# RMSNorm with repeated rows: gamma loaded on the loads' own queue, and one VectorE copy in two

## The chip, the cores and the metric

The kernel runs on one core of a Trainium2 chip. The core has five engines with an instruction stream each: TensorE (PE, unused here), VectorE (DVE), ScalarE (ACT), GpSimd (POOL) and SyncE (SP), and sixteen DMA engines that move data between the chip's main memory (HBM) and the on-chip memory of 128 partitions. A DMA is issued from a queue of an engine, SP's (q1 in the profile) or ACT's (q10) here, and is cut into packets that are spread over the DMA engines. Each engine works through its instructions in order and waits on semaphores for the others.

The metric is the time of one execution on the device, in microseconds (us), as the median of several runs.

## What is computed

```python
# x: 8 x 512 x 2048 float32, gamma: 2048 float32
x_rep = np.repeat(x, 2, axis=1)
rms = np.sqrt((x_rep ** 2).mean(axis=-1, keepdims=True) + 1e-6)
return ((x_rep / rms) * gamma[None, None, :]).astype(np.float32)
```

Every row of 2048 values is divided by its root mean square, multiplied by gamma, and written out twice in a row. 33.5 MB are read and 67.1 MB written.

## The kernel before

All 4096 rows are taken in four loads of 1024 rows: each partition gets 8 consecutive rows (64 KB, one contiguous piece of HBM). One load feeds two stores; a store writes 4 rows of each partition, twice each, so again 64 KB per partition. That makes 4 loads and 8 stores, twelve transfers of 128 pieces of 64 KB, all issued by SP in one queue.

On chip there is one tile y of 24 rows per partition, in three areas of 8 rows called `first`, `second` and `third`. `four(n, constants)` handles two loads, and is called twice. It issues load n into rows 4 to 11, then runs `constants()` (which does work in the first call only), then issues load n+1 into `third`. Four groups follow, each of 4 rows per partition:

- `squares` (L57): ACT squares each row and sums it up (L63), then takes the root (L67).
- `scale` (L70): DVE takes the reciprocal (L73), then one operation per row multiplies by it and by `gamma_b` (L75), writing into the even places of the group's area.
- `repeat` (L80): a copy of the even places into the odd ones (L82), by ACT or DVE.
- `store` (L52): SP issues the store (L53).

The first group of a call is done in two halves of 2 rows; its first half is copied by ACT, its second by DVE. In the second group (`second`), ACT copies the second half and DVE the first half, one copy of 4096 elements per partition (L102). The third and fourth group are copied by ACT alone. An area is written again only when the store that reads it has landed: load 2 waits for the third store (and, in the same queue, load 3 for the fourth).

The order of instructions on every engine is the order in which the program issues them (a manual schedule). SP's queue is thus load 0, load 1, four stores, load 2, load 3, four stores; here loads and stores are counted from 0.

`constants()` (L120) brings gamma in and spreads it over the partitions. It issues on ACT's queue one DMA of 16 pieces of 125 values (500 B, L121) and three DMAs of one piece of 16 values (64 B, L127). They go to one partition of y, into rows that no load fills but the first group's scaling writes later; so the first store also waits for these DMAs. Then POOL broadcasts the 2000 values to all partitions of `gamma_b` (L131) and the last 48 (L135). DVE sets the constant eps (L136), and ACT takes a root of it (L139), which also loads ACT's table.

Of the kernel before, what the change touches and what calls it, by code (L numbers as in the profile page):

```python
# [1 line left out]

# [4 lines left out]


@with_exitstack
def kernel(  # L10
    ctx: ExitStack,
    tc: tile.TileContext,
    x: bass.AP,
    gamma: bass.AP,
    out: bass.AP,
):
    nc = tc.nc
    P = nc.NUM_PARTITIONS
    f32 = mybir.dt.float32
    Act = mybir.ActivationFunctionType  # L20
    Alu = mybir.AluOpType

    B, S, D = x.shape
    Bo, So, Do = out.shape
    R = So // S
    assert R == 2 and D == Do and B == Bo and So == S * R
    eps = 1e-6
    inv_d = 1.0 / float(D)


    K = 4
    N = B * S
    ntiles = N // (P * K)
    assert N % (P * K) == 0 and ntiles == 8
    H = 2
    x_t = x.rearrange("b s d -> (b s) d").rearrange("(n p k) d -> n p k d", p=P, k=H * K)
    out_t = out.rearrange("b s d -> (b s) d").rearrange("(n p h j) d -> n h p (j d)", p=P, h=H, j=K * R)

    singles = ctx.enter_context(tc.tile_pool(name="singles", bufs=1))
    rows = ctx.enter_context(tc.tile_pool(name="rows", bufs=1))  # L40
    junk = ctx.enter_context(tc.tile_pool(name="junk", bufs=1, space=bass.MemoryType.PSUM))
    small = ctx.enter_context(tc.tile_pool(name="small", bufs=4))

    y = rows.tile([P, 3 * K * R, D], f32, name="y")
    first, second, third = 0, K * R, 2 * K * R

    def load(n, at):
        nc.sync.dma_start(out=y[:, at : at + H * K, :], in_=x_t[n])  # L50

    def store(n, h, to):  # L52
        nc.sync.dma_start(  # L53
            out=out_t[n, h], in_=y[:, to : to + K * R, :].rearrange("p j d -> p (j d)")
        )

    def squares(at, rows):  # L57

        n = len(rows)
        ss = small.tile([P, n], f32, name=f"ss{n}")  # L60
        for c, k in enumerate(rows):
            sq = junk.tile([P, D], f32, name="sq")
            nc.scalar.activation(  # L63
                out=sq[:], in_=y[:, at + k, :], func=Act.Square, accum_out=ss[:, c : c + 1]
            )
        rms = small.tile([P, n], f32, name=f"rms{n}")
        nc.scalar.activation(out=rms[:], in_=ss[:], func=Act.Sqrt, scale=inv_d, bias=eps_t[:])  # L67
        return rms

    def scale(at, to, rows, rms):  # L70
        n = len(rows)
        rstd = small.tile([P, n], f32, name=f"rstd{n}")
        nc.vector.reciprocal(out=rstd[:], in_=rms[:])  # L73
        for c, k in enumerate(rows):
            nc.vector.scalar_tensor_tensor(  # L75
                out=y[:, to + R * k, :], in0=y[:, at + k, :], scalar=rstd[:, c : c + 1],
                in1=gamma_b[:], op0=Alu.mult, op1=Alu.mult,
            )

    def repeat(to, k0, k1, copy):  # L80
        y_r = y[:, to + R * k0 : to + R * k1, :].rearrange("p (k r) d -> p k r d", r=R)
        copy(out=y_r[:, :, 1, :], in_=y_r[:, :, 0, :])  # L82

    ctx.enter_context(tc.manual_schedule())

    half = K // 2
    up, down = list(range(K)), list(range(K - 1, -1, -1))

    def four(n, constants):


        load(n, first + K)
        constants()
        load(n + 1, third)
        for rows in (up[:half], up[half:]):
            scale(first + K, first, rows, squares(first + K, rows))
        repeat(first, 0, half, nc.scalar.copy)
        repeat(first, half, K, nc.vector.tensor_copy)
        store(n, 0, first)
        scale(second, second, down, squares(second, down))  # L100
        repeat(second, half, K, nc.scalar.copy)
        repeat(second, 0, half, nc.vector.tensor_copy)  # L102
        store(n, 1, second)
        roots = [squares(third + h * K, up) for h in range(H)]
        scale(third, first, up, roots[0])
        repeat(first, 0, half, nc.scalar.copy)
        repeat(first, half, K, nc.scalar.copy)
        store(n + 1, 0, first)
        scale(third + K, third, up, roots[1])
        repeat(third, 0, K, nc.scalar.copy)  # L110
        store(n + 1, 1, third)

    gamma_b = singles.tile([P, D], f32, name="gamma_b")
    G, E = 16, 3
    C = D // G - E
    gamma_s = y[0:1, 0:2, :].rearrange("p k (c d) -> p (k c) d", c=G // 2)
    gamma_t = y[0:1, 2, :]
    eps_t = singles.tile([P, 1], f32, name="eps_t")

    def constants():  # L120
        nc.scalar.dma_start(  # L121
            out=gamma_s[0:1, :, :C],
            in_=gamma[: G * C].rearrange("(p c d) -> p c d", p=1, c=G),
        )
        for c in range(E):
            at = G * C + c * G
            nc.scalar.dma_start(  # L127
                out=gamma_t[0:1, c * G : (c + 1) * G],
                in_=gamma[at : at + G].partition_broadcast(1),
            )  # L130
        nc.gpsimd.partition_broadcast(  # L131
            out_ap=gamma_b[:, : G * C].rearrange("p (c d) -> p c d", c=G),
            in_ap=gamma_s[0:1, :, :C],
        )
        nc.gpsimd.partition_broadcast(out_ap=gamma_b[:, G * C :], in_ap=gamma_t[0:1, : E * G])  # L135
        nc.vector.memset(eps_t, eps)  # L136

        root = singles.tile([P, 1], f32, name="root")[:]
        nc.scalar.activation(out=root, in_=eps_t[:], func=Act.Sqrt)  # L139

    four(0, constants)
    four(2, lambda: None)


# [1 line left out]
_INS = ['x', 'gamma']  # L146
_OUTS = [((8, 1024, 2048), 'float32')]


# [23 lines left out]
```

## Time and profile before

| what | value |
|---|---|
| median of 3 runs (lowest to highest) | 238.42 us (238.42 to 239.19) |
| profiled execution, its own time | 238.52 us |
| its span, first to last instruction | 236.3 us |
| busy: DVE, ACT, POOL | 84.4, 110.2, 2.8 us (36%, 47%, 1% of the span) |
| moved by DMA | 100.68 MB, mean 426 GB/s |
| load 0 issued, landed | 0.72, 22.70 us |
| gamma landed: the 16 pieces, the three small DMAs | 10.59; 15.43, 20.27, 22.88 us |

The profile is of one execution. Its page gives, line by line, the busy time of the engines, the DMA queues (packets, MB, and the time of their packets as a share of sixteen engines' span), a chain of work followed back from the last instruction, and groups of instructions: line, engine, operation, output<-input, count, then busy us and mean ns of one, then the idle time of the engine just before them and what ended most of it. A timeline gives start and duration in us, the engine, and in square brackets the idle time before and its releaser. A table by stretches gives for each stretch its length, then busy time (and count) of DVE, ACT and POOL, the clock of TensorE, the DMA engines' share and GB/s. The trace behind it also has each DMA packet with start, duration and size, and the moment at which each engine's share of a DMA was reported as landed; a completion packet of 4 B follows the data of each DMA on each engine.

### The profile page before, as it was taken

The page shows a single profiled execution, that of the slowest core. Times are in us where ns is not written, and L with a number is a line of the kernel's source. Part 1 is how long each engine was busy: PE and PEld are TensorE (multiplying, and loading weights), DVE is VectorE, ACT ScalarE, POOL GpSimd, SP SyncE. Part 2 cuts the span into 40 slices and gives each one's busy share as a digit, 9 for nine tenths or more (in the row PEclk, how much of TensorE's full clock was granted, in tenths as well). Part 3 has the DMA queues.
Part 4 walks back from the last instruction along what each step waited for, and adds up shares of the span by engine and source line. Part 5 has one row for each costly group of instructions (what it writes and reads, how often), then busy time and mean ns, then how long its engine had stood idle before and what let it go on. Part 6 is the DMA issues. An engine that isn't in the chain of part 4 may idle for free.

```text
span 236.3 us, 225 instructions
## 1 busy us (share of the span) xinstructions
DVE 84.4 (36%) x47; ACT 110.2 (47%) x86; POOL 2.8 (1%) x6
## 2 busy tenths in 40 slices
DVE  0000396594699500000000007929919992000000
ACT  2001989479998470000000049991999957400000
POOL 0110000000000000000000000000000000000000
DMA  9898989989898989999898988989898988989894
GB/s 355 356 532 355 521 366 466 422 388 499 355 532 356 521 366 466 422 399 488 355 532 355 510 377 377 510 355 532 355 532 355 510 377 388 499 355 532 355 532 177
DMA packets 1767, 100.68 MB, mean 426 GB/s; under 512 B 230, under 2 KB 230, under 8 KB 230
## 3 DMA queue, kind: packets, MB, share of 16 engines
q1 hardware_dynamic: 1728, 100.66, 98.7%
q10 hardware_dynamic: 38, 0.01, 0.0%
q14 instruction: 1, 0.01, 0.0%
HBM read 33.56 MB, written 67.11 MB: 426 GB/s over the span
## 4 chain that ended last, share of the span: by engine, by line
DMA 45%; ACT 26%; DVE 12%; issue 2%; DVEq 0%
DMA y<-in_x_dram 26%; DMA out_dram<-y 19%; ACT sq L63 15%; DVE y L75 12%; ACT y L82 11%; ACT rms L67 1%; DVE rstd L73 0%; DVEq L75 0%
## 5 line engine op out<-in xcount | busy, mean ns | idle before, releaser
L63 ACT ACTIVATE sq<-y 128x2048 f32<-128x2048 f32 x32 | 60.1, 1878 | 71.1 <-DMA y<-in_x_dram 70.4
L75 DVE SCALAR_TENSOR_TENSOR y<-y,rstd,gamma_b 128x2048 f32<-128x2048 f32 x32 | 73.8, 2348 | 1.6 <-DMA out_dram<-y 1.0
L82 ACT COPY y<-y 128x4096 f32<-128x4096 f32 (+1 forms) x10 | 42.6, 4283 | 19.1 <-DVE y L75 18.3
L73 DVE RECIPROCAL rstd<-rms 128x4 f32<-128x4 f32 (+1 forms) x10 | 1.7, 170 | 109.2 <-ACT rms L67 109.2
L82 DVE COPY y<-y 128x4096 f32<-128x4096 f32 x4 | 9.2, 2294 | 0.1
L63 ACT ACTIVATION_READ_ACCUMULATOR sq<-y 128x1 f32 x32 | 6.0, 186 | 0.0
L67 ACT ACTIVATE rms<-ss,eps_t 128x4 f32<-128x4 f32 (+1 forms) x10 | 3.0, 297 | 0.3
L139 ACT ACT_TABLE_LOAD x1 | 1.3, 1283 | 2.6 <-issue 2.6
L131 POOL PARTITION_BROADCAST gamma_b<-y x1 | 2.2, 2243 | 10.2 <-DMA y<-in_gamma_dram 10.2
L135 POOL PARTITION_BROADCAST gamma_b<-y x1 | 0.3, 323 | 10.2 <-DMA y<-in_gamma_dram 10.2
L136 DVE MEMSET eps_t<- 128x1 f32 x1 | 0.1, 59 | 0.8 <-PEq L157 0.8
L139 ACT ACTIVATE root<-eps_t 128x1 f32<-128x1 f32 x1 | 0.2, 202 | 0.0
L157 POOL MEMSET const-bfloat16-1.0<- 128x1 bf16 x1 | 0.1, 101 | 0.0
L157 POOL MEMSET const-uint8-127<- 128x1 uint8 x1 | 0.1, 101 | 0.0
L157 POOL MEMSET const-float32-0.0<- 128x1 f32 x1 | 0.1, 98 | 0.2 <-issue 0.2
L157 POOL MEMSET const-float32-1.0<- 128x1 f32 x1 | 0.1, 99 | 0.0
## 6 DMA issues: line engine op xcount, KB each, us to landing
out_dram<-y SPq DMA_DIRECT2D x8, 24.7
y<-in_x_dram SPq DMA_DIRECT2D x4, 31.4
y<-in_gamma_dram ACTq DMA_DIRECT2D x3, 0.1 KB
y<-in_gamma_dram ACTq DMA_DIRECT2D x1, 7.8 KB, 9.9
```

The source lines that it names most:

```text
L63: nc.scalar.activation(out=sq[:], in_=y[:, at + k, :], func=Act.Square, accum_out=ss[:, c : c + 1])
L67: nc.scalar.activation(out=rms[:], in_=ss[:], func=Act.Sqrt, scale=inv_d, bias=eps_t[:])
L73: nc.vector.reciprocal(out=rstd[:], in_=rms[:])
L75: nc.vector.scalar_tensor_tensor(out=y[:, to + R * k, :], in0=y[:, at + k, :], scalar=rstd[:, c : c + 1], in1=gamma_b[:], op0=Alu.mult, op ...
L82: copy(out=y_r[:, :, 1, :], in_=y_r[:, :, 0, :])
L131: nc.gpsimd.partition_broadcast(out_ap=gamma_b[:, : G * C].rearrange("p (c d) -> p c d", c=G), in_ap=gamma_s[0:1, :, :C],)
L135: nc.gpsimd.partition_broadcast(out_ap=gamma_b[:, G * C :], in_ap=gamma_t[0:1, : E * G])
L136: nc.vector.memset(eps_t, eps)
L139: nc.scalar.activation(out=root, in_=eps_t[:], func=Act.Sqrt)
L157: nc = _bacc.Bacc("TRN2", target_bir_lowering=False, num_devices=1)
```

## The change

Gamma's DMAs move from ACT's queue to SP's, so between load 0 and load 1. There are four, each of 16 pieces of 32 values (128 B): every DMA takes a quarter of each of sixteen parts of gamma. They go straight to partition 0 of `gamma_b`, and one broadcast spreads that partition over all. The rows of y are no longer used for gamma.

In the second call of `four` (loads 2 and 3), DVE's one copy for the second group becomes two copies of one row each, 2048 elements. The first call keeps its single copy.

```diff
-    def four(n, constants):
+    def four(n, constants, step):
...
-        repeat(second, 0, half, nc.vector.tensor_copy)
+        for k in range(0, half, step):
+            repeat(second, k, k + step, nc.vector.tensor_copy)
...
-    G, E = 16, 3
-    C = D // G - E
-    gamma_s = y[0:1, 0:2, :].rearrange("p k (c d) -> p (k c) d", c=G // 2)
-    gamma_t = y[0:1, 2, :]
...
     def constants():
-        nc.scalar.dma_start(
-            out=gamma_s[0:1, :, :C],
-            in_=gamma[: G * C].rearrange("(p c d) -> p c d", p=1, c=G),
-        )
-        for c in range(E):
-            at = G * C + c * G
-            nc.scalar.dma_start(
-                out=gamma_t[0:1, c * G : (c + 1) * G],
-                in_=gamma[at : at + G].partition_broadcast(1),
-            )
-        nc.gpsimd.partition_broadcast(
-            out_ap=gamma_b[:, : G * C].rearrange("p (c d) -> p c d", c=G),
-            in_ap=gamma_s[0:1, :, :C],
-        )
-        nc.gpsimd.partition_broadcast(out_ap=gamma_b[:, G * C :], in_ap=gamma_t[0:1, : E * G])
+        G = 16
+        g_in = gamma.rearrange("(p c d) -> p c d", p=1, c=G)
+        g_to = gamma_b[0:1, :].rearrange("p (c d) -> p c d", c=G)
+        w = D // G // 4
+        for c in range(0, D // G, w):
+            nc.sync.dma_start(out=g_to[:, :, c : c + w], in_=g_in[:, :, c : c + w])
+        nc.gpsimd.partition_broadcast(out_ap=gamma_b[:], in_ap=gamma_b[0:1, :])
         nc.vector.memset(eps_t, eps)
...
-    four(0, constants)
-    four(2, lambda: None)
+    four(0, constants, half)
+    four(2, lambda: None, 1)
```

More of the change, by code (lines that the diff above doesn't have):

```diff
@@ L113 @@
     gamma_b = singles.tile([P, D], f32, name="gamma_b")
-    G, E = 16, 3
-    C = D // G - E
-    gamma_s = y[0:1, 0:2, :].rearrange("p k (c d) -> p (k c) d", c=G // 2)
-    gamma_t = y[0:1, 2, :]
     eps_t = singles.tile([P, 1], f32, name="eps_t")
     def constants():
-        nc.scalar.dma_start(
-            out=gamma_s[0:1, :, :C],
-            in_=gamma[: G * C].rearrange("(p c d) -> p c d", p=1, c=G),
-        )
-        for c in range(E):
-            at = G * C + c * G
-            nc.scalar.dma_start(
-                out=gamma_t[0:1, c * G : (c + 1) * G],
-                in_=gamma[at : at + G].partition_broadcast(1),
-            )
-        nc.gpsimd.partition_broadcast(
-            out_ap=gamma_b[:, : G * C].rearrange("p (c d) -> p c d", c=G),
-            in_ap=gamma_s[0:1, :, :C],
-        )
-        nc.gpsimd.partition_broadcast(out_ap=gamma_b[:, G * C :], in_ap=gamma_t[0:1, : E * G])
+        G = 16
[5 more added lines that the diff above has]
+        nc.gpsimd.partition_broadcast(out_ap=gamma_b[:], in_ap=gamma_b[0:1, :])
         nc.vector.memset(eps_t, eps)
-        root = singles.tile([P, 1], f32, name="root")[:]
-        nc.scalar.activation(out=root, in_=eps_t[:], func=Act.Sqrt)
-    four(0, constants)
-    four(2, lambda: None)
+        root = singles.tile([P, 1], f32, name="root")
+        nc.scalar.activation(out=root[:], in_=eps_t[:], func=Act.Sqrt)
+    four(0, constants, half)
+    four(2, lambda: None, 1)
 _INS = ['x', 'gamma']
```

## Prediction

> **What bounds the kernel.** I read the page first, then busy time by stretches, then the timeline around the first use of gamma, and last the packet records of the trace. From the page:
>
> ```profile
> span 236.3 us, 225 instructions
> ...
> q1 hardware_dynamic: 1728, 100.66, 98.7%
> q10 hardware_dynamic: 38, 0.01, 0.0%
> ...
> DMA 45%; ACT 26%; DVE 12%; issue 2%; DVEq 0%
> ...
> L82 DVE COPY y<-y 128x4096 f32<-128x4096 f32 x4 | 9.2, 2294 | 0.1
> ...
> L131 POOL PARTITION_BROADCAST gamma_b<-y x1 | 2.2, 2243 | 10.2 <-DMA y<-in_gamma_dram 10.2
> L135 POOL PARTITION_BROADCAST gamma_b<-y x1 | 0.3, 323 | 10.2 <-DMA y<-in_gamma_dram 10.2
> ```
>
> q1 is SP's queue with all loads and stores: its packets fill 98.7% of sixteen DMA engines, 0.987 x 236.3 = 233.2 us on each. The packet records give the same sum: 12 transfers of 128 pieces of 64 KB are 96 per engine, nearly all of 2.418 us, so 232.1 us. The chain gives DMA only 45% and ACT and DVE 38%, which would mislead; by stretches (DMA share and GB/s stand last):
>
> ```profile
> 0.00:22.70 22.70, 0.06 (x1) 1.49 (x2) 2.43 (x5) 1.00 0.99 416
> 22.70:39.20 16.50, 11.85 (x7) 15.59 (x14) 0.32 (x1) 1.00 1.02 441
> 39.20:138.80 99.60, 30.33 (x16) 38.75 (x29) 0.00 (x0) 1.00 1.00 432
> ```
>
> Where the chain runs through ACT and DVE (22.7 to 39.2), the DMA engines are as full as elsewhere: the compute is only just in time and makes no gap. (A share over 1 comes from packets counted whole where they begin.) So the end is the first packet's start (1.74 us), 233 us of gapless packets, the last landing (235.50) and 0.8 us of closing. Only three things move it: packet time added to or taken from an engine, a gap in the stream, or another start. The profiled execution took 238.52 us, 2.2 more than its span; the median of the runs shown is 0.1 less, 238.42.
>
> **The nearest point at which compute could open a gap** is the first store:
>
> ```profile
> 22.72 1.88 ACT L63 ACTIVATE sq<-y 128x2048 f32<-128x2048 f32 x1 [18.64 <-DMA y<-in_x_dram]
> 23.07 0.32 POOL L135 PARTITION_BROADCAST gamma_b<-y  x1 [10.15 <-DMA y<-in_gamma_dram]
> ...
> 26.79 0.29 ACT L67 ACTIVATE rms<-ss,eps_t 128x2 f32<-128x2 f32 x1
> ...
> 27.12 0.17 DVE L73 RECIPROCAL rstd<-rms 128x2 f32<-128x2 f32 x1 [26.27 <-ACT rms L67]
> 27.38 2.35 DVE L75 SCALAR_TENSOR_TENSOR y<-y,rstd,gamma_b 128x2048 f32<-128x2048 f32 x1
> ```
>
> ```profile
> 36.88 2.29 DVE L82 COPY y<-y 128x4096 f32<-128x4096 f32 x1
> ...
> 39.24 0.35 SPq L53 DMA_DIRECT2D out_dram<-y  x1
> ```
>
> Load 0 lands at 22.70, the first use of gamma_b starts at 27.38 behind two squares and their root, and DVE then works on to the copy whose end lets store 0 be issued at 39.24. The second load's last packets end, engine by engine, between 41.0 and 41.67, and store 0's follow at once. Load 0 itself needed 1.02 us (first engine) to 1.88 us (last) from issue to packet. So store 0 has 41.0 - 39.24 - 1.02 = 0.7 us to spare on the first engine and 41.67 - 39.24 - 1.88 = 0.55 on the last: about 0.6 us. A delay of DVE beyond that becomes a gap, and no later stage wins it back.
>
> **The change, part by part.**
>
> *Removed: gamma's four DMAs on ACT's queue and the second broadcast.* Each of the 16 pieces of 500 B took 26 ns on its engine and its completion packet 9: 35 ns on each engine; the three 64 B pieces took 11 + 9 each on one engine, 60 ns more there. Their issues held ACT from 0.72 to 2.56; ACT then idles until 22.72 (18.6 us), so the earlier table load is worth nothing. Store 0's wait for the old staging rows goes too; it was over at 22.88, under the wait for DVE that ends at 39.2. The first stores' own data is late next, unchanged.
>
> *Added: four DMAs of 16 pieces of 128 B between load 0 and load 1.* On SP they delay the issue of load 1 (now 1.16). ACT's gamma issues took 0.21 to 0.67 each, so four take 0.8 to 2.7 and load 1 goes out by 4 us; its first packet is due at 21.66, and all later issues stand behind it, the first at 39. Hidden, with 15 us of cover. On the engines, one piece and one completion packet per DMA: 128 B lies between the 11 ns of 64 B and the 26 ns of 500 B, so 4 x (11 to 26 + 9) = 0.08 to 0.14 us. Less the 0.035 removed, +0.045 to +0.105 us on every engine, straight on the path. I take **+0.1**, the upper end.
>
> *Moved: gamma lands later, because its pieces stand behind load 0.* Load 0's completion packets ran at 21.65 to 22.31; with 0.14 more the last of gamma's runs by 22.46. From completion packet to landing the trace has 0.39 us (load 0) and 0.74 (the third 64 B piece): landing at 22.9 to 23.2. POOL started 0.08 and 0.19 after its landings. One broadcast of 2048 elements: the rows are 2.243 us for 2000 and 0.323 for 48, so (2.243 - 0.323)/1952 = 0.98 ns per element and 2.29 us; ends are 2.24 (the larger one alone) and 2.57 (both added). It ends between 25.2 and 26.0, 1.4 to 2.2 us ahead of 27.38. Behind it on POOL nothing waits; on DVE the first scaling would, and all after it. Cost **0**; if gamma landed d later than forecast, d - 1.4 to d - 2.2 would reach DVE, and 0.6 less than that the end.
>
> Here the Trainium skill speaks against the change. "DMA: Bandwidth & Descriptors" (Anatomy of one DMA) gives a small DMA about 2.0 us of fixed cost, mostly the wait for the write's receipt, and under Rules for kernel authors says to coalesce small transfers. If four stood in series, an estimate from that page is 8 us: gamma at 30.7, DVE 5.7 us late, the end 5 us later. The trace has the third 64 B piece at 22.132, its completion packet at 22.145 and the next 64 KB packet at 22.151 on the same engine: the landing came 0.74 us after, but the engine did not wait for it.
>
> *The first transfer's start.* Load 0 is issued at the same 0.72 us as ACT's first gamma DMA, and its packets start over 1.74 to 2.60. Should the two issues have shared something, the start may gain, at most that spread, 0.86 us; a loss has no reason, since load 0 is still the first on its queue. I take 0: no row shows a start without a neighbour.
>
> *One copy into two (second store of the second group only).* The copy of 4096 elements takes 2.29 us. Two of 2048: between 2.29 (nothing fixed) and 4.59 (nothing saved). The smallest DVE instruction of the chain, a reciprocal of 2 columns, takes 0.16, so I take +0.1 to +0.2. That store is issued at 171.91 and its packets follow on between 176.68 and 177.21: 4.8 less 1.0 to 1.9 of issue leaves about 3 us, more than even the 2.3 of the worst end. DVE next idles to 176.86. Cost **0**.
>
> **Sum:** 238.52 + 0.1 = 238.6 for the profiled execution; 0.1 less for the median as before: **238.5 us**.
>
> **Rivals.**
>
> *A read exposed at each small piece (slower).* Load 0's first packets took 2.51 to 3.445 instead of 2.418, up to 1.03 us of exposed read; the last packets ahead of load 2, where stores turn to loads, took up to 3.031, 0.61 more. If each small piece emptied an engine's pipeline that way, four in a row would cost 2.4 to 4.1 us: 240.9 to 242.6. It decides from two exposures on (1.2 us); a single one gives 239.1. Against it: where 500 B pieces ran between 64 KB packets of load 0, these kept their 2.418. For it: no trace has small pieces one after another in this queue.
>
> *Gamma in turns with load 1.* On ACT's queue one 64 B DMA came 4.85 us after the other, two 64 KB packets of the loads between. If that held here, gamma would land 19.4 us late, DVE would start some 17 late, and the time be about 255. Against it: within q1 all of load 0's completion packets ran before load 1, issued 0.4 us later.
>
> *The spreading fails.* If all 64 pieces went to one engine, that engine would take 64 x (11 to 26) ns, 0.7 to 1.7 us more, and the slowest engine sets the end: 239.2 to 240.2. Against it: the old DMA of 16 pieces landed by sixteen separate events.
>
> *The start gains:* 237.6 to 238.2.
>
> **How the numbers follow.** Forecast 0.80; start gains 0.05; one exposure 0.04; two to four 0.07; spreading fails 0.03; turns 0.01. The bound of 0.5% (1.2 us) is about what a measurement of this kernel can tell from no change. Slower by more: 0.07 + 0.01 + half of 0.03, 0.10. Faster by more: the greatest gain is 0.9, so only with a lucky median, 0.02. Within: 0.88. The range runs from 238.0 (part of the start's gain) to 239.7 (one exposure, half of the failed spreading, and a median like the highest run shown, 239.19, with some to spare).
>
> **What would show it.** Right: q1 with 128 packets more at still about 98.7%; 64 KB packets at 2.418 about 22 us; the broadcast of about 2.3 us starting near 23.2; the first scaling still at 27.4, store 0 at 39.2. Wrong: load 1's packets beginning well over 0.14 us after load 0's completion, or a first scaling that waits for POOL; then the step on the engines' small packets, or that on the landing, has failed.

## The result, and the profile after

The changed kernel takes **239.67 us** (median of 10 runs, 238.99 to 240.47); the kernel before, beside it, 238.44 (10 runs, 238.40 to 239.19). The ratio is 1.0044, 95% interval 1.0034 to 1.0053: about 1.05 us slower (the two medians differ by 1.23). The profiled execution took 239.94 us with a span of 238.1. From its page:

```profile
span 238.1 us, 224 instructions
...
q1 hardware_dynamic: 1856, 100.67, 98.3%
...
DMA 46%; ACT 26%; DVE 13%; issue 1%; DVEq 0%
...
L82 DVE COPY y<-y 128x4096 f32<-128x4096 f32 (+1 forms) x5 | 9.2, 1865 | 0.1
...
L124 POOL PARTITION_BROADCAST gamma_b<-gamma_b x1 | 2.3, 2292 | 23.3 <-DMA gamma_b<-in_gamma_dram 23.3
```

q1 has the 128 packets more that were forecast and q10 is gone. The broadcast takes 2.29 us. The share of q1 fell from 98.7% to 98.3% while the span grew: the stream is a little less dense somewhere. By stretches, again cut at load 0's landing and store 0's issue, and at load 2's landing:

```profile
0.00:22.86 22.86, 0.06 (x1) 1.49 (x3) 0.19 (x4) 1.00 0.99 413
22.86:39.45 16.59, 11.86 (x7) 15.68 (x14) 2.29 (x1) 1.00 1.02 442
39.45:140.70 101.25, 30.33 (x16) 38.65 (x29) 0.00 (x0) 1.00 0.99 425
```

The first two are nearly as they were, together 0.25 us longer. The third is 1.65 longer and holds most of what changed: load 2 lands at 140.70 instead of 138.79. The timeline around gamma shows that no wait for gamma's values began it:

```profile
22.86 1.88 ACT L63 ACTIVATE sq<-y 128x2048 f32<-128x2048 f32 x1 [20.63 <-DMA y<-in_x_dram]
23.73 2.29 POOL L124 PARTITION_BROADCAST gamma_b<-gamma_b  x1 [23.30 <-DMA gamma_b<-in_gamma_dram]
...
27.25 0.17 DVE L73 RECIPROCAL rstd<-rms 128x2 f32<-128x2 f32 x1 [26.40 <-ACT rms L67]
27.57 2.35 DVE L75 SCALAR_TENSOR_TENSOR y<-y,rstd,gamma_b 128x2048 f32<-128x2048 f32 x1 [0.15 <-DVE rstd L73]
```

The broadcast is over at 26.02, before the reciprocal that the first scaling needs anyway, and the releaser named at 27.57 is that reciprocal. Most of the loss is one line of the chain in order of time (start, length, what). First the kernel before, then the changed one:

```profile
76.20 23.79 DMA out_dram<-y
100.00 38.79 DMA y<-in_x_dram
```

```profile
76.36 23.90 DMA out_dram<-y
100.28 40.42 DMA y<-in_x_dram
```

The second line runs from store 2's landing to load 2's. In between the queue holds store 3 and load 2, two transfers of 8 packets per engine: 16 x 2.418 = 38.7 us. The kernel before loses 0.1 there, the changed one 1.7. It is the only place in the program where stores are followed by loads; I call it **the turn**. The packet records show how: in the changed kernel the last packets of store 3 take up to 3.53 us and the first of load 2 up to 3.11, on some engines and not on others, so that load 2's sixteen landings spread over 138.64 to 140.70, where before they lay within 138.30 to 138.79. Once apart, the engines do not come together again (the last landings lie within 235.92 to 237.28): the latest one does its five remaining transfers in 96.6 us, 5 x 8 packets of 2.418 being 96.7, and sets the end (last landing 237.28; before 235.50).

The profiled executions add up: +0.27 up to store 2's last landing (99.99 to 100.26), +1.64 at the turn (load 2's last landing 140.70 - 100.26 against 138.79 - 99.99), -0.13 after it: span +1.78. But the time grew by 1.42 only. The time less the span is 238.52 - 236.32 = 2.20 us before and 239.94 - 238.11 = 1.83 after: **0.37 us came back outside the span**, on which the prediction had no term.

### The profile page after: what moved, and what is told of

Its sections match the earlier page's. It is cut to its first block, busy times and chain, and to the rows that moved or that the text cites. A ratio compares the mean times of both kernels' runs of the same rounds, so it can differ in the third digit from the quotient of the medians.

```text
span 238.1 us, 224 instructions
## 1 busy us (share of the span) xinstructions
DVE 84.5 (35%) x48; ACT 110.2 (46%) x86; POOL 2.5 (1%) x5
## 3 DMA queue, kind: packets, MB, share of 16 engines
q1 hardware_dynamic: 1856, 100.67, 98.3%
## 4 chain that ended last, share of the span: by engine, by line
DMA 46%; ACT 26%; DVE 13%; issue 1%; DVEq 0%
DMA y<-in_x_dram 26%; DMA out_dram<-y 19%; ACT sq L63 15%; DVE y L75 13%; ACT y L82 10%; ACT rms L67 1%; DVE rstd L73 0%; DVEq L75 0%
## 5 line engine op out<-in xcount | busy, mean ns | idle before, releaser
L82 DVE COPY y<-y 128x4096 f32<-128x4096 f32 (+1 forms) x5 | 9.2, 1865 | 0.1
L124 POOL PARTITION_BROADCAST gamma_b<-gamma_b x1 | 2.3, 2292 | 23.3 <-DMA gamma_b<-in_gamma_dram 23.3
```

The costliest lines, as they stand in the source:

```text
L124: nc.gpsimd.partition_broadcast(out_ap=gamma_b[:], in_ap=gamma_b[0:1, :])
```

## The experiments

All ratios are to the kernel before, run beside each; intervals are 95%. "Turn" is the time from store 2's landing to load 2's in the profiled execution. The fourth column counts single runs by their span; of the kernel before, 2 of 98 had one over 237.2 us.

| run | ratio (interval) | turn, us | runs with span over 237.2 | time less span |
|---|---|---|---|---|
| before | 1 | 38.79 | 2 of 98 | 2.20 |
| changed | 1.0044 (1.0034 to 1.0053) | 40.42 | 9 of 10 | 1.83 |
| gamma's part alone | 1.0050 (1.0034 to 1.0066) | 40.06 | 5 of 6 | 2.20 |
| split copy alone | 0.9982 (0.9974 to 0.9991) | 38.96 | 0 of 11 | 1.82 |
| gamma in one packet | 1.0017 (1.0004 to 1.0031) | 38.62 | 1 of 12 | 2.20 |
| two gamma DMAs | 1.0033 (1.0019 to 1.0047) | 38.63 | 6 of 12 | 2.22 |
| four on ACT's queue | 1.0022 (1.0004 to 1.0040) | 40.62 | 6 of 12 | 1.86 |
| eight gamma DMAs | 1.0167 (1.0154 to 1.0180) | 38.53 | see below | 1.66 |
| before + four small DMAs | 1.0172 (1.0159 to 1.0186) | 38.56 | see below | 2.20 |
| changed + fifth DMA, 8 x 16 | 1.0015 (1.0006 to 1.0023) | 38.73 | 1 of 11 | 1.97 |
| changed + fifth DMA, 16 x 8 | 1.0008 (0.9998 to 1.0019) | 38.79 | 1 of 11 | 1.96 |
| before + one VectorE instruction | 0.9974 (0.9958 to 0.9990) | 38.72 | 0 of 11 | 1.85 |
| before + three | 0.9979 (0.9963 to 0.9995) | 38.88 | 1 of 12 | 1.64 |
| changed + small read at the turn | 1.0027 (1.0011 to 1.0044) | 40.77 | 7 of 12 | 1.97 |

One execution of each kernel was traced. Leaving out the two kernels with 1.0167 and 1.0172, the four traced executions with a span over 237.2 us have a turn of 40.06 or more, the eight others one of at most 38.96. So for the runs without a trace I take a span over 237.2 as the loss at the turn; that is inferred, not seen.

**Gamma's part alone.**

```diff
-    four(2, lambda: None, 1)
+    four(2, lambda: None, half)
```

> Gamma's part alone: VectorE's copy of the second group stays one copy in both calls. The changed kernel took 1.0044 times the kernel before, about 1.05 us. Theory A, that the four small DMAs on the loads' queue cost it (0.15 to 0.25 us where they stand, the rest at the one place where stores turn to loads, between store 3 and load 2): 1.003 to 1.005. Theory B, that the split copy shifts something in the second call: 1.000 to 1.001.

Measured 1.0050, and in its chain again:

```profile
100.03 40.06 DMA y<-in_x_dram
```

The slowdown, all of it, belongs to gamma's part. In this execution the span is 1.65 us longer: up to store 2's landing (100.03) it was as fast as the kernel before (100.00), 1.27 us came at the turn, and 0.35 after it, where one of load 3's last packets took 2.92 us.

**The split copy alone.** The kernel before, with the loop of the change around VectorE's copy and step 1 in the second call.

> The kernel before with only VectorE's copy split in the second call. Theory A: 1.000, since about 3 us of cover lie under store 5. Theory B: 1.003 to 1.005.

Neither theory had this: 0.9982, a gain. The span did not shrink (236.5), but the time less the span fell to 1.82. Store 5's issue was well covered, as predicted; in the changed kernel, too, the two copies together take only 0.07 us more than the one of 2.29 (start, length):

```profile
171.46 2.36 DVE L82 COPY y<-y 128x2048 f32<-128x2048 f32 x2
```

**Gamma in one DMA on the loads' queue.** The edit leaves one DMA instead of four:

```diff
-        w = D // G // 4
+        w = D // G
```

> The changed kernel with gamma in one DMA of 16 pieces of 512 B on the loads' queue instead of four of 128 B: two packets per engine instead of eight. Theory A in its plain form (each small DMA costs its share): 1.001, a quarter of the loss. Theory A in its other form (anything in this queue ahead of the later transfers disturbs the turn from stores to loads): 1.003 to 1.005. Theory B: 1.003 to 1.005.

1.0017; eleven of its twelve runs lie at 238.82 to 239.14, one at 240.62. But the DMA was not the one that the expectation describes. Uncut, gamma is one contiguous piece, and the trace has it as a single packet of 8 KB on one engine (309 ns) instead of 16 pieces of 512 B. The page counts two packets more than the 1728 of the twelve transfers, that one and its completion packet:

```profile
q1 hardware_dynamic: 1730, 100.67, 98.6%
```

Its 0.4 us (0.1 to 0.7 by the interval) do not come from the turn, which lost nothing (38.62): the last landing of load 1 is already 0.20 us later than in the kernel before, that of store 2 still 0.22. So something small between load 0 and load 1 does not bring the loss by itself; what one DMA spread over all the engines does was not tried.

**Gamma's four DMAs on ACT's queue.**

```diff
-            nc.sync.dma_start(out=g_to[:, :, c : c + w], in_=g_in[:, :, c : c + w])
+            nc.scalar.dma_start(out=g_to[:, :, c : c + w], in_=g_in[:, :, c : c + w])
```

> The changed kernel with its four gamma DMAs issued on ACT's queue; one broadcast, and the split copy, as in the changed kernel. Theory A: 1.000 to 1.001, the loads' queue holds only the twelve large transfers again. Theory B: 1.003 to 1.005. If the staging rows in y or the second broadcast mattered (theory C): 1.003 to 1.005 too, which the run of the split alone tells from theory B.

1.0022; half its runs have a span over 237.2, and the profiled one lost 1.9 us at the turn (40.62). Theory A, that it is the loads' queue, falls: four such DMAs on the other queue do it too, here in fewer of the runs. The runs without the loss have spans of 236.5 to 236.9, beside a median of 236.4 for the kernel before: the vanished staging rows and second broadcast cost a few tenths of a microsecond at most.

**Gamma in eight DMAs, and four small DMAs added to the kernel before.** The first has `w = D // G // 8`; the second leaves gamma on ACT's queue and adds

```diff
+        g_in = gamma.rearrange("(p c d) -> p c d", p=1, c=G)
+        g_to = y[0:1, 3, :].rearrange("p (c d) -> p c d", c=G)
+        w = D // G // 4
+        for c in range(0, D // G, w):
+            nc.sync.dma_start(out=g_to[:, :, c : c + w], in_=g_in[:, :, c : c + w])
```

> The changed kernel with gamma in eight DMAs of 16 pieces of 64 B on the loads' queue. So far one such DMA gave 1.0017, four 1.0044; in the runs with a loss a few DMA engines come out of the turn from store 3 to load 2 late (load 2 lands up to 1.9 us later than its first engine), and the end follows the latest engine. Theory N (the number of small DMAs ahead of the turn makes it worse): 1.005 to 1.009, load 2's landings spread over 2 us or more. Theory P (only the offsets of the engines against each other at the turn matter, the number does not): anywhere from 1.002 to 1.006, not above the changed kernel.

> The kernel before, its gamma on ACT's queue as it was, with the four small DMAs of the change added on the loads' queue between load 0 and load 1; they write a row of y that is written over later, so nothing uses them. Theory N: 1.004 to 1.005 with the spread of load 2's landings of the changed kernel, since the added DMAs alone do it. If it is the missing traffic on ACT's queue at the start that does it: 1.000 to 1.001.

Both lost 4 us, 1.0167 and 1.0172, and both for a reason that I had not asked about, so that neither answers its question. SP's waits up to 30 us, first with eight DMAs, then with four more:

```profile
SPq L123 <- DMA y<-in_x_dram: 17.0, 1, 17.0
```

```profile
SPq L140 <- DMA y<-in_gamma_dram: 7.5, 1, 7.5
SPq L50 <- DMA y<-in_x_dram: 11.9, 1, 11.9
```

The completion semaphores in the trace are eight, taken in turn; a ninth DMA has to wait until the one that had its semaphore has landed. With eight DMAs the last of gamma's waits for load 0; with four more the last of these waits for the 16 pieces on ACT's queue, and load 1 for load 0. In these two kernels ten DMAs stand ahead of the first store instead of six, so load 1, issued at 3.67 us in the changed kernel, was issued at 23.19 and 22.92, behind load 0's landing. The engines ran empty (in the second kernel load 1's first packets began at 23.89, those of the kernel before at 21.66), the first packets were slow again (2.8 to 3.5 us), and load 1's last packets, with store 0 already in the queue, took 3.3 to 4.1 us on all sixteen engines. At the turn, however, these two lost nothing: 38.53 and 38.56.

**Two gamma DMAs.** `w = D // G // 2`.

> The changed kernel with gamma in two DMAs of 16 pieces of 256 B on the loads' queue. Theory N: 1.002 to 1.003, between one DMA and four. Theory P: anywhere from 1.001 to 1.005.

1.0033, and the runs fall into two heaps: six at 238.84 to 239.08, six at 239.77 to 240.34. The turn's loss then looks like something that an execution has or has not, and not like a fixed price. The profiled execution is of the lower heap and had none (38.63); none of the upper heap was traced.

**A fifth DMA, written in two ways.** Both have 128 pieces of 64 B more on the loads' queue behind gamma's four. Written 8 x 16 they were meant to go to eight engines and pull these apart from the others; written 16 x 8 (`a=8, b=8` and `a=16, b=8` below) they were meant to go to all.

```diff
+        nc.sync.dma_start(
+            out=y[0:1, 0:2, :].rearrange("p k (a b c) -> p (k a) b c", a=4, b=16)[:, :, :, :16],
+            in_=gamma.rearrange("(p a b c) -> p a b c", p=1, a=8, b=16),
+        )
```

> The changed kernel with one more DMA on the loads' queue after gamma's four: 8 x 16 pieces of 64 B, so that eight of the sixteen DMA engines get 16 small packets more (some 0.16 to 0.2 us) and the other eight none; it writes rows of y that are written over later. It pulls the engines apart before the turn. Theory P (engines close together at the turn disturb each other): 1.001 to 1.003, load 2's landings within 0.9 us. Theory N: 1.005 to 1.007, as the changed kernel plus the 0.2 us.

> As the staggered kernel, with the same fifth DMA of 128 pieces of 64 B, but cut 16 x 8, so that each of the sixteen engines gets 8 small packets and none is pulled apart from another. Theory P (being pulled apart spared the staggered kernel the loss at the turn): 1.004 to 1.006, load 2's last landing 1 us or more later than 38.7 us after store 2's last landing. If a fifth DMA or the later issue of load 1 spared it: 1.001 to 1.002.

The two are the same kernel. Both patterns name the same 128 pieces at the same addresses, and in both traces the fifth DMA runs on all sixteen engines and lands by sixteen events. The page of each has the same line, 144 packets more than the changed kernel: 128 pieces and sixteen completion packets.

```profile
q1 hardware_dynamic: 2000, 100.68, 98.6%
```

With the engines taken in order of time, there are 2.54 to 2.55 us from the start of load 0's last packet to that of load 1's first on fifteen of them, in the one trace as in the other (the last has 2.67 and 2.79); an engine without the added pieces would have kept the 2.48 of the changed kernel. So no engine was pulled apart, and the comparison of staggered and even was not made. What there is instead is one kernel measured twice: 1.0015 and 1.0008, turns of 38.73 and 38.79, a span over 237.2 in 2 of 22 runs.

For engines that are not pulled apart theory P (engines close together disturb each other) had forecast 1.004 to 1.006, and theory N (more small DMAs, more loss) 1.005 to 1.007: both fall in this form. The traces say the same of closeness as such: store 2's sixteen landings, the last before the turn, lie within 0.47 to 0.76 us of each other in the four executions with the loss, and within 0.43 to 0.86 in the ten without. The kernel with the fifth DMA rarely had the loss; the changed kernel was not run again beside it. What the fifth DMA adds is eight small packets on each engine between load 0 and load 1. In the first trace load 0's last and load 1's first packets lost 0.39 us per engine against 2.418 each, in the second 0.45; at the turn both then lost 0.1 or less.

**One and three tiny VectorE instructions more in the kernel before.** eps is set twice, or four times:

```diff
         nc.vector.memset(eps_t, eps)
+        nc.vector.memset(eps_t, eps)
```

> The kernel before with the setting of eps on VectorE done twice: one tiny instruction (59 ns, at 0.8 us, while VectorE idles) more, and no split copy. In all ten kernels traced so far the profiled execution's time less its span is 2.20 to 2.22 us with 61 recorded instructions on VectorE, 1.82 to 1.86 with 62, 1.97 with 63, 1.66 with 64. Theory L (the gain of the split copy alone comes from the length of VectorE's instruction stream, outside the span): time less span 1.83, ratio 0.998 to 0.999. Theory S (it comes from the split copy itself, in the second call): 2.20 and 1.000.

> The kernel before with eps set four times: three tiny VectorE instructions more and nothing else. Theory L: time less span 1.66, as in the kernel with 64 recorded VectorE instructions, so the ratio 0.9975 to 0.9985 and below the split copy alone. Theory S: 1.000.

0.9974 and 0.9979, time less span 1.85 and 1.64, both as theory L has it (the first ratio is a little below its 0.998 to 0.999, which its interval takes in); theory S falls. The start of VectorE's timeline where eps is set twice:

```profile
0.79 0.06 DVE L136 MEMSET eps_t<- 128x1 f32 x1 [0.79 <-PEq L158]
0.91 0.06 DVE L137 MEMSET eps_t<- 128x1 f32 x1
```

An instruction of 59 ns in an idle stretch makes the kernel faster by as much as the split copy does. With the split copy alone these are the fastest of all: medians of 238.28 and 238.14 us beside 238.70 for the kernel before.

**A small read at the turn.** The changed kernel, with one DMA ahead of load 2:

```diff
+        if n == 2:
+            nc.sync.dma_start(
+                out=y[0:1, 0, :].rearrange("p (c d) -> p c d", c=16)[:, :, :32],
+                in_=gamma.rearrange("(p c d) -> p c d", p=1, c=16)[:, :, :32],
+            )
         load(n, first + K)
```

> The changed kernel with one small DMA more, 16 pieces of 128 B of gamma, on the loads' queue between store 3 and load 2, so at the turn from stores to loads; it writes a row of y that is written over later. In the changed kernel load 2's latest engine landed 40.4 us after store 2's latest, where two transfers of 19.32 would take 38.6: 1.8 us lost at this turn. Theory R (the first reads of load 2 stand exposed behind the last writes, and the small pieces would meet that instead): 1.000 to 1.002, landing within 38.9 us. If the turn's loss does not hang on what is read first: 1.004 to 1.005, and 39.5 us or more.

1.0027, 40.77 us from store 2's landing (100.09) to load 2's (140.86). The small pieces had landed by 120.35 and spared load 2 nothing in this execution. Seven of twelve runs have a span over 237.2, against nine of ten without the small read: too few to call a difference. Theory R falls in the form in which I put it.

## Why the prediction was right or wrong

- **The forecast was +0.1 us; measured is +1.05 by the ratio. The median of 239.67 lies inside the range (238.0 to 239.7) by 0.03 us, and that is luck: the reasons were neither those of the sum nor those of the range.** The upper end had been made of an exposed read, a failed spreading and a high median, and neither of the first two happened. Two unforeseen terms of opposite sign made the difference: gamma's part alone +1.2 us (0.8 to 1.6 by its interval), the split copy alone -0.4 (-0.6 to -0.2).
- **"What bounds the kernel" was right.** The end is the stream of packets on the latest engine, and neither kernel gains or loses by its compute. Store 4 in the changed kernel shows it from the other side: load 2's late engines held its issue back from 155.26 to 157.19, the early engines stood empty for about half a microsecond (19.83 us between their landings of load 3 and store 4 instead of 19.35), and it cost nothing, because the latest engine, which sets the end, never waited.
- **The added small packets were priced a little too high.** Each piece took 13 ns and its completion packet 9, which adds up to 4 x 22 = 0.09 us, inside 0.08 to 0.14; but their records overlap. From the start of load 0's last packet to that of load 1's first are 2.48 us instead of 2.42, so the four cost an engine 0.06. One after another they left no gap: on the latest engine load 1's first packet followed load 0's completion after 0.07 us. The rival of a read exposed at each piece is out.
- **The moved gamma was nearly right.** It landed from 22.79 to 23.53 instead of 22.9 to 23.2. Load 0 itself was 0.13 later, and the term from completion packet to landing was too small: 0.39 to 0.74 in the sum, 1.00 us (22.53 to 23.53) for the last of the four. The broadcast ended at 26.02 (forecast to 26.0) and the first scaling did not wait for it. The Trainium skill's "DMA: Bandwidth & Descriptors" (Anatomy of one DMA) gives its 2 us for one DMA issued from GpSimd. These four were issued from SP, and adding four fixed costs in series, as the estimate in the prediction does, does not fit the trace: the last landings of load 0 and of the four stand at 22.83, 23.00, 23.18, 23.35 and 23.53, 0.18 us apart.
- **The step that failed is "packet time added to or taken from an engine", the sum over the added packets alone.** I took the other 1536 packets as fixed at 2.418 us. The prediction had the row against it: the last packets ahead of load 2 took up to 3.031 us in the kernel before. I used it to price a rival elsewhere, and did not ask whether that spot itself would change. It did: in the four profiled executions that had the loss the turn took 1.3 to 2.0 us more on the latest engine than in the kernel before.
- **"One copy into two: cost 0" missed a gain.** Store 5's cover was right and the copies cost 0.07 us, but one VectorE instruction more took 0.37 us off the time outside the span. In all fourteen kernels the time less the span follows the number of recorded VectorE instructions (waits included, counted in the trace): 2.20 to 2.22 us at 61, 1.82 to 1.86 at 62, 1.96 to 1.97 at 63, 1.64 to 1.66 at 64. It holds for the single runs too: 1.77 to 1.88 in all runs of the split copy alone and of the kernel with one instruction more, 2.14 to 2.27 in the 98 of the kernel before. What makes it so, no run shows.
- **"The start gains" did not happen**: the first packet began at 1.73 us (before 1.74). "The spreading fails" and "in turns with load 1" did not happen either.

**What stays open** is why gamma's four DMAs make the turn's loss frequent. Shown is where it is, that gamma's part alone brings it, and that it comes with either queue; two DMAs have it in half of the runs, a single packet on one engine in 1 of 12, five DMAs in 2 of 22. The queue, the number of small DMAs as such, the engines' closeness before the turn, and what is read first there do not explain it, as far as these runs go. The traces add one thing: it begins with the last packets of store 3. That store's sixteen landings lie within 0.22 to 0.50 us of each other in the ten executions without the loss, and within 0.69 to 1.19 in the four with it. That an early wait between load 0 and load 1 spares a later one would fit the kernel with the fifth DMA and the two in which load 1 was late, but the kernel before and the one with gamma in one packet have no such wait and rarely the loss. It was not tried by itself.

## What to carry to other kernels

When a kernel is bound by a saturated DMA queue, look in the packet records for places where packets already take longer than the rest, such as a turn from stores to loads, and take several executions there: a small edit elsewhere can change how often that place loses, and the latest engine carries the loss to the end. Count DMAs against completion semaphores before adding some: here the ninth waited for an earlier one to land. Count the packets of every DMA that you vary, too: two patterns that look different can be the same DMA, and an uncut one can go to a single engine. And before crediting an edit with a few tenths of a microsecond, subtract the span from the time, and try one idle instruction instead.

## What the runs showed of the hardware

- Four small DMAs (16 pieces of 128 B each) queued one behind the other between 64 KB packets cost each engine 0.06 us in all and land 0.18 us apart.
- At the one turn from stores to loads the latest of the sixteen engines loses between nothing and 2.1 us, differently from trace to trace. In the kernel before, nearly all the other packets of 64 KB took 2.418 us; load 0's first took up to 3.45, and a few others up to 2.60.
- Load 1's last packets took 3.3 to 4.1 us, on all engines, in the two kernels where store 0 was issued 1.9 us or more before these packets began; both kernels also had load 1 late. In the other kernels these packets had begun when store 0 was issued, or began within 0.06 us, and none took over 2.78.
- The time outside the span goes with the number of VectorE instructions, by up to 0.56 us, and one or three instructions added by themselves changed it by 0.35 and 0.56.
